# A hybrid block on one core: eight row products on TensorE in four modulation blocks, one scaling on ScalarE, and the roots of both LRU directions side by side

## The chip, the core and the metric

The kernel runs on one core of a Trainium2 chip. Five engines of that core work in parallel, each in the order of its own queue: TensorE (PE; its weight loads are counted as PEld), VectorE (DVE), ScalarE (ACT), GpSimd (POOL) and SyncE (SP), which issues most of the transfers. The metric is the device time of one execution in microseconds.

## The reference, cut to what matters

One layer, sequence 1024, model width 1024, batch 1, all in float32. `c` gives six modulation vectors; the first two, shift and scale, act on the normalised input.

```python
mod = jnp.dot(jax.nn.silu(c), w_mod[l]) + b_mod[l]
shift1, scale1, gate1, shift2, scale2, gate2 = jnp.split(mod[:, None, :], 6, axis=-1)
h = rms_norm(x, g_norm1[l]) * (1.0 + scale1) + shift1
proj = jnp.dot(h, w_in[l])
x_lru, z_lru, q, k, v = jnp.split(proj, SPLITS, axis=-1)
xc = conv(x_lru)                                  # 4 taps along the sequence
h_fwd = rg_lru(xc, w_a[0], ..., reverse=False)
h_bwd = rg_lru(xc, w_a[1], ..., reverse=True)
y_lru = (h_fwd + h_bwd) * jax.nn.gelu(z_lru)
y_att = diff_attention(q, k, v, ...)              # q and k are rms-normed per head first
x = x + gate1 * jnp.dot(jnp.concatenate([y_lru, y_att], -1), w_out[l])
x = x + gate2 * expert_choice_ffn(rms_norm(x, g_norm2[l]) * (1 + scale2) + shift2, ...)
```

The recurrence of one direction is `h = a * h_before + u`, with two gates `r` and `i` from block-diagonal products:

```python
log_a = LRU_C * r * jax.nn.log_sigmoid(lam)
a = jnp.exp(log_a)
u = jnp.sqrt(-jnp.expm1(2.0 * log_a)) * (i * xc)
```

## The kernel before

Products in float32 are made of rounded parts: `hh` and `hl` are the high and low part of a block of `h`, `w..h` and `w..l` those of a weight, and each product is three passes (high by high, high by low, low by high).

**The front.** The 1024 columns of `h` are cut into eight blocks of 128. For block k, shift and scale are a product of the 1024 values of `silu(c)` with 256 columns of `w_mod`, loaded as two tiles `wm` of four rows of weights each. `m_mm(k)` lets PE do the first `RP[k]` of the eight row products, into the PSUM tile `mp`. `m_sum(k)` brings the rest in on DVE: with `RP[k] == 8` one COPY of `mp` to `acc` (L303), otherwise four products with addition (L305), of which the last writes `acc`. `m_red(k)` sums `acc` over the partitions on PE (tile `pm`), `m_col(k)` makes the columns `acol` and `shc` of it (L315, L317), and `h_make(k)` scales: `hh` on ACT, the plain scaling (`h_2` for block 2) on DVE (L326) where k is in `KH` and else on ACT, and the difference `hl` (L329), on POOL for all blocks but the last. `x_mm` multiplies the blocks with the first 256 columns of `w_in` into `pjx`. The order of PE, DVE and ACT in this stretch is that in which the code is written (a manual schedule): `m_mm(k + 2)` and `m_sum(k + 2)`, the products of block k, then `m_red`, `m_col` and `h_make` of block k + 2.

**The LRU.** From `pjx` the convolution makes tiles `xc` (one for 128 channels, four in all, indexed by ct), and `do_lru(ct)` does both directions of one: `xch` and `xcl`, the parts of `xc`; gates `pg` on PE and `tg` on ACT (Tanh); `tt` (Tanh), the decay `a` in place in the first `tg` (Exp) and its Square `sqa` on ACT; two products on DVE (L515, L516); then for each direction the root of `tt` on ACT, a product on POOL (L521, out `tg`) and a scan over the sequence on DVE (L523 forward, L525 backward), and at last the addition of both (L528). Here a scheduler orders each engine's instructions. Whenever the next function on ACT is not in the loaded set, an ACT_TABLE_LOAD stands ahead of it.

**Between them** run the q and k projections, `proj_qk`: a projection `pjq` or `pjk` on PE; its Square `sqk` on ACT, a reduction `rk` on DVE (L578), a root on ACT, a reciprocal (L580) and a product `nk` (L582) on DVE, and then eight transposes of `nk` on PE (`pbk`, L589), from which `hk` on ACT and `lk` on DVE (`hq` and `lq` for q, L596) follow. The projections' weights are split: `wi_0h`, `wi_1h` on ACT, `wi_0l`, `wi_1l` on POOL or DVE (L142). The PSUM pools of `pj` and of `pg` have two tiles each, so a projection can begin only when the one before the last has been read.

**After that** come attention, the output projection, and the experts, which take the second half of the time.

Of the kernel before, what the change touches and what calls it, by code (L numbers as in the profile page):

```python
# [12 lines left out]
AF = mybir.ActivationFunctionType  # L13
# [44 lines left out]
KS0 = 1  # L58
KLT = 4
KM = 3  # L60
RP = (8, 8, 4, 4, 4, 4, 4, 4)
KW = 7
KV = (7,)
KH = (0, 1, 2, 7)
KB = (0, 1, 2, 7)
CAP = 128
RPAD = 56
# [15 lines left out]
def tile_block(ctx: ExitStack, tc, x, cols, w_mod, b_mod, w_in, wa, wx, lam_qk, relT, w_out, g2, w_router,  # L83
# [5 lines left out]
    def act(out, in_, func=AF.Copy, **kw):  # L89
        return A.activation(out=out, in_=in_, func=func, **kw)  # L90

    def mm(out, lhsT, rhs, start, stop):
        return T.matmul(out, lhsT=lhsT, rhs=rhs, start=start, stop=stop)  # L93
# [46 lines left out]
    def split(src, hi, lo, eng=None):  # L140
        act(hi, src)
        return (eng or V).tensor_tensor(out=lo, in0=src, in1=hi.bitcast(F32), op=ALU.subtract)  # L142
# [151 lines left out]
    def m_mm(k):  # L294
        mps[k] = psb.tile([P, 2, P], F32, tag="pj", bufs=2, name=f"mp{k}")
        for r in range(RP[k]):
            g = 32 * (r % 4)
            mm(mps[k][g:g + 32], scz[:, r, :], wm[k, r // 4][:, r % 4], r < 4, r + 4 >= RP[k])

    def m_sum(k):  # L300
        accs[k] = sm1.tile([P, 2, P], F32, tag="acc", bufs=4, name=f"acc{k}_0")
        if RP[k] == KT:
            V.tensor_copy(accs[k], mps[k])  # L303
        for r in range(RP[k], KT):
            V.scalar_tensor_tensor(out=accs[k] if r == KT - 1 else mps[k], in0=wm[k, r // 4][:, r % 4], scalar=sc[:, r:r + 1],  # L305
# [13 lines left out]
    def h_make(k):  # L319
# [4 lines left out]
        i_ = act(a, xT[k], AF.Identity, scale=ac, bias=sh)  # L324
        if k in KH:
            V.tensor_scalar(out=b32, in0=xT[k], scalar1=ac, scalar2=sh, op0=ALU.mult, op1=ALU.add)  # L326
# [116 lines left out]
    def lt_(name, shape=None, dt=F32):  # L443
        return lru.tile(shape or [P, S], dt, tag="l", bufs=NL, name=name)
# [46 lines left out]
    def do_lru(ct):  # L491
        xc = xc_[ct]
        xh = lt_(f"xch{ct}", None, F32R)
        xl = lt_(f"xcl{ct}", None, F32R)
        split(xc, xh, xl, V if ct in LV else G_)
        hs, st = [], []
        for d in range(2):
            pre = []
            for gi in range(2):
                pg = psb.tile([P, 1024], F32, tag="pg", bufs=2, name=f"pg{ct}_{d}_{gi}")  # L500
                i = d * 4 + ct
                for wi_, (w_, xv) in enumerate(((bdh, xh), (bdl, xh), (bdh, xl))):
                    for n in range(2):
                        mm(pg[:, n * 512:(n + 1) * 512], w_[gi][:, i, :], xv[:, n * 512:(n + 1) * 512], wi_ == 0, wi_ == 2)
                tg = lt_(f"tg{ct}_{d}_{gi}")
                act(tg, pg, AF.Tanh, scale=0.5, bias=hb[:, gi * 8 + i:gi * 8 + i + 1])
                pre.append(tg)
            ta, ti = pre
            i = d * 4 + ct
            tt = lt_(f"tt{ct}_{d}")  # L510
            act(tt, ta, AF.Tanh, scale=nkap[:, i:i + 1], bias=nkap[:, i:i + 1])
            act(ta, ta, AF.Exp, scale=kap[:, i:i + 1], bias=kap[:, i:i + 1])
            sq = lt_(f"sqa{ct}_{d}")
            act(sq, ta, AF.Square)
            V.scalar_tensor_tensor(out=tt, in0=sq, scalar=1.0, in1=tt, op0=ALU.add, op1=ALU.mult)  # L515
            tis.append(V.scalar_tensor_tensor(out=ti, in0=ti, scalar=1.0, in1=xc, op0=ALU.add, op1=ALU.mult))  # L516
            st.append((ta, ti, tt))
        for d in range(2):
            ta, ti, tt = st[d]
            act(tt, tt, AF.Sqrt, scale=0.25)  # L520
            G_.tensor_tensor(out=ti, in0=ti, in1=tt, op=ALU.mult)  # L521
            if d == 0:
                V.tensor_tensor_scan(out=tt, data0=ta, data1=ti, initial=0.0, op0=ALU.mult, op1=ALU.add)  # L523
            else:
                V.tensor_tensor_scan(out=tt[:, ::-1], data0=ta[:, ::-1], data1=ti[:, ::-1], initial=0.0,  # L525
                                     op0=ALU.mult, op1=ALU.add)
            hs.append(tt)
        V.tensor_tensor(out=hs[0], in0=hs[0], in1=hs[1], op=ALU.add)  # L528
        hs_[ct] = hs[0]
# [112 lines left out]
    mod_rest(0, 1)  # L642
    behind.reverse()
    do_lru(0)
    wq1 = load_in(1280, G_)
    mod_rest(0, 2)
# [3 lines left out]
    mod_rest(0, 4)  # L650
    proj_qk(wq1, 0, 1)
    do_lru(1)
    mod_rest(0, 5)
    wz0 = load_in(512, G_)
# [35 lines left out]
    mod_rest(1, 4)  # L690
    behind.append(convs[1])
    proj_v(wv0, 0, vt[0:2], lambda _: do_lru(2), VA)
    mod_rest(1, 5)
    behind.append(tis[-1])
# [786 lines left out]
```

## Time and the profile before

| | |
|---|---|
| Time, median of 3 runs | 1165.89 us (1162.89 to 1166.04) |
| The profiled execution: time, span | 1167.24 us, 1165.5 us |
| Busy share of the span: PE, PEld, DVE, ACT, POOL | 96%, 80%, 82%, 68%, 39% |
| Mean granted clock of TensorE | 0.978 |
| Waits of PE from 20 to 320 us | 2.2, 2.0 and 1.2 us, and three of 0.4 us or less |

The span is counted from the first instruction to the last. Times in the rows are microseconds from the start of the span, unless they are marked otherwise. A granted clock of 1.0 is full speed (2.4 GHz), 0.50 is half. In a timeline, rows of equal form that follow each other are put together (x3), and in brackets stands how long the engine was idle before, and what ended that.

### The profile page before, as it was taken

The page shows a single profiled execution, that of the slowest core. Times are in us where ns is not written, and L with a number is a line of the kernel's source. Part 1 is how long each engine was busy: PE and PEld are TensorE (multiplying, and loading weights), DVE is VectorE, ACT ScalarE, POOL GpSimd, SP SyncE. Part 2 cuts the span into 40 slices and gives each one's busy share as a digit, 9 for nine tenths or more (in the row PEclk, how much of TensorE's full clock was granted, in tenths as well). Part 3 has the DMA queues.
Part 4 walks back from the last instruction along what each step waited for, and adds up shares of the span by engine and source line. Part 5 has one row for each costly group of instructions (what it writes and reads, how often), then busy time and mean ns, then how long its engine had stood idle before and what let it go on. Part 6 is the DMA issues. An engine that isn't in the chain of part 4 may idle for free.

```text
span 1165.5 us, 17852 instructions
## 1 busy us (share of the span) xinstructions
PE 1113.3 (96%) x6303; PEld 935.2 (80%) x6303; DVE 960.6 (82%) x1258; ACT 795.1 (68%) x1051; POOL 457.9 (39%) x528
## 2 busy tenths in 40 slices
PE   5999999999999999999379999999999999999996
PEld 4799998888899998777358888888888888888885
DVE  7686767884699995655779999999999999999995
ACT  7539382384588785543448888787888787888784
POOL 5683331133144463553634332444332444332410
PEclk9899999999999999999679999999999999999998
DMA  9753637615684217336889999999999999999911
GB/s 338 232 167 106 238 106 252 218 37 130 197 227 104 76 37 255 127 127 217 309 313 326 394 394 383 393 391 387 397 394 392 367 391 403 400 392 386 389 33 18
DMA packets 146992, 304.33 MB, mean 261 GB/s; under 512 B 16972, under 2 KB 43724, under 8 KB 146900
## 3 DMA queue, kind: packets, MB, share of 16 engines
q1 hardware_dynamic: 135008, 279.99, 66.4%
q0 software_dynamic: 5488, 19.45, 6.4%
q10 hardware_dynamic: 6408, 3.77, 1.1%
q8 instruction: 49, 0.80, 0.3%
q14 instruction: 39, 0.32, 0.1%
HBM read 277.95 MB, written 25.21 MB: 260 GB/s over the span
## 4 chain that ended last, share of the span: by engine, by line
PE 88%; DVE 4%; issue 3%; SPq 2%; DMA 1%; ACT 1%; POOLq 0%; POOL 0%; DVEq 0%; ACTq 0%
PE ab L93 28%; PE y L93 14%; PE mix L93 7%; PE pv L93 5%; PE sc L93 5%; PE pjk L93 4%; PE pjv L93 4%; PE pjz L93 4%; PE pjx L93 4%; PE pjq L93 3%; PE pw L820 2%; PE pg L93 2%; SPq L288 1%; PE pf L1365 1%; PE pe L1274 1%
## 5 line engine op out<-in xcount | busy, mean ns | idle before, releaser
L1265 POOL TENSOR_SCALAR oh<-iot,slot 128x128 bf16<-128x128 bf16 x120 | 144.1, 1215 | 252.3 <-PE pf L1365 252.3
L93 PE MATMUL ab<-wh,xeh 128*128 128x512 f32 x512 | 202.2, 395 | 0.3 <-ACT xeh L90 0.3
L93 PE MATMUL ab<-wh,xel 128*128 128x512 f32 x512 | 199.6, 390 | 0.0
L93 PE MATMUL ab<-wl,xeh 128*128 128x512 f32 x512 | 157.7, 389 | 0.0
L93 PEld LDWEIGHTS ab<-wl,xeh 128*128 128x128 f32 x512 | 96.1, 188 | 20.4
L93 PEld LDWEIGHTS ab<-wh,xel 128*128 128x128 f32 x512 | 96.2, 188 | 19.4 <-DVE xel L1278 0.5
L93 PEld LDWEIGHTS ab<-wh,xeh 128*128 128x128 f32 x512 | 96.0, 188 | 19.5 <-ACT xeh L90 0.5
L142 DVE TENSOR_TENSOR wl<-w_0r,wh 128x1024 fp32r<-128x1024 f32 x79 | 96.9, 1226 | 10.5 <-ACT wh L90 0.4
L90 ACT ACTIVATE wh<-w_0r 128x1024 fp32r<-128x1024 f32 x81 | 85.9, 1062 | 24.3 <-PE ab L93 14.9
L142 DVE TENSOR_TENSOR wl<-w_3r,wh 128x1024 fp32r<-128x1024 f32 x79 | 96.7, 1224 | 6.3
L90 ACT ACTIVATE wh<-w_1r 128x1024 fp32r<-128x1024 f32 x79 | 83.6, 1059 | 23.0 <-PE ab L93 18.8
L90 ACT ACTIVATE wh<-w_3r 128x1024 fp32r<-128x1024 f32 x79 | 83.9, 1063 | 22.2 <-PE ab L93 17.4
L142 DVE TENSOR_TENSOR wl<-w_2r,wh 128x1024 fp32r<-128x1024 f32 x80 | 96.3, 1220 | 2.4 <-ACT wh L90 1.1
L90 ACT ACTIVATE wh<-w_2r 128x1024 fp32r<-128x1024 f32 x80 | 84.8, 1060 | 19.7 <-PE ab L93 17.8
L142 DVE TENSOR_TENSOR wl<-w_1r,wh 128x1024 fp32r<-128x1024 f32 x78 | 92.5, 1219 | 3.6 <-ACT wh L90 1.6
L774 DVE CUSTOM_DVE_ANT_0 p<-sc,bias 128x1024 f32<-128x1024 f32 x64 | 77.8, 1217 | 10.7 <-PE sc L93 10.6
L93 PE MATMUL y<-wh,htl 128*128 128x512 f32 x256 | 82.9, 395 | 0.0
L93 PE MATMUL y<-wh,hth 128*128 128x512 f32 x256 | 81.1, 396 | 0.0
L93 PE MATMUL y<-wl,hth 128*128 128x512 f32 x256 | 79.5, 391 | 0.0
L90 ACT ACTIVATE p<-p,stat 128x1024 f32<-128x1024 f32 x60 | 68.4, 1151 | 0.3 <-DVE stat L774 0.3
L93 PEld LDWEIGHTS pv<-v,wt 128*128 128x128 f32 x512 | 61.7, 192 | 2.5
L93 PE MATMUL pv<-v,wt 128*128 128x128 f32 x512 | 62.1, 275 | 0.0
(466 smaller groups left out, 2843.8 us busy)
## 6 DMA issues: line engine op xcount, KB each, us to landing
w_0r<-in_w_dram SPq DMA_DIRECT2D x81, 512.0 KB, 5.0
w_1r<-in_w_dram SPq DMA_DIRECT2D x79, 512.0 KB, 5.9
w_2r<-in_w_dram SPq DMA_DIRECT2D x78, 512.0 KB, 6.0
w_3r<-in_w_dram SPq DMA_DIRECT2D x77, 512.0 KB, 8.9
wr<-in_w_mod_dram SPq DMA_DIRECT2D x32, 512.0 KB, 4.4
wi<-in_w_in_dram SPq DMA_DIRECT2D x18, 512.0 KB, 3.4
w_5r<-in_w_dram SPq DMA_DIRECT2D x17, 512.0 KB
wm<-in_w_mod_dram SPq DMA_DIRECT2D x32, 256.0 KB, 4.4
```

The lines of the kernel that those rows point to most:

```text
L90: return A.activation(out=out, in_=in_, func=func, **kw)
L93: return T.matmul(out, lhsT=lhsT, rhs=rhs, start=start, stop=stop)
L142: return (eng or V).tensor_tensor(out=lo, in0=src, in1=hi.bitcast(F32), op=ALU.subtract)
L288: lds.append(SY.dma_start(out=w[:, :, g, :], in_=w_mod[rh * 512:(rh + 1) * 512, c0:c0 + P].rearrange("(r p) c -> p r c", p=P)))
L774: V.tensor_tensor_reduce(out=p_, in0=scp[g, j], in1=prs[h][0][:, b0:b0 + S], op0=ALU.add, op1=ALU.min, scale=1.0, scalar=3.0e38, accum_out ...
L820: T.transpose(pw[:, b * P:(b + 1) * P], pt_[g, 0][:, kt * P:(kt + 1) * P], ident)
L1265: G_.tensor_scalar(out=oh[:, t, :], in0=iot, scalar1=slot[:, e, t:t + 1], scalar2=None, op0=ALU.is_equal)
L1274: T.transpose(pt[:, b * P:(b + 1) * P], xe[:, (kq * 4 + b) * P:(kq * 4 + b + 1) * P], ident)
L1365: T.transpose(pt[:, b * P:(b + 1) * P], sa[:, b * P:(b + 1) * P], ident)
```

## The change

There are three edits. `RP` is 8 for blocks 2 and 3 too, so PE does all eight row products of these and DVE copies. `KH` loses block 2, so ACT makes its plain scaling. In `do_lru` the roots of both directions are issued after the Square of the second direction.

```diff
-RP = (8, 8, 4, 4, 4, 4, 4, 4)
+RP = (8, 8, 8, 8, 4, 4, 4, 4)
 KW = 7
 KV = (7,)
-KH = (0, 1, 2, 7)
+KH = (0, 1, 7)
...
             sq = lt_(f"sqa{ct}_{d}")
-            act(sq, ta, AF.Square)
+            i_sq = act(sq, ta, AF.Square)
             V.scalar_tensor_tensor(out=tt, in0=sq, scalar=1.0, in1=tt, op0=ALU.add, op1=ALU.mult)
...
         for d in range(2):
             ta, ti, tt = st[d]
-            act(tt, tt, AF.Sqrt, scale=0.25)
+            with tc.issue_after(i_sq.ins):
+                act(tt, tt, AF.Sqrt, scale=0.25)
             G_.tensor_tensor(out=ti, in0=ti, in1=tt, op=ALU.mult)
```

On DVE, at the front, the order changes as follows (`mp_430` belongs to block 2, `mp_461` or `mp_462` to block 3; a line without a sign is in both).

```order
 L326 TENSOR_SCALAR h_1_418<-xT_121,acol,shc 128x1024
-L305 SCALAR_TENSOR_TENSOR mp_430<-wm_1_222,sc,mp_430 128x256 x3
-L305 SCALAR_TENSOR_TENSOR acc_0_435<-wm_1_222,sc,mp_430 128x256
-L315 SCALAR_TENSOR_TENSOR acol<-pm_444,bs_112,col 128x1
-L317 TENSOR_TENSOR shc<-pm_444,col 128x1
-L326 TENSOR_SCALAR h_2_451<-xT_121,acol,shc 128x1024
-L305 SCALAR_TENSOR_TENSOR mp_461<-wm_1_228,sc,mp_461 128x256 x3
-L305 SCALAR_TENSOR_TENSOR acc_0_466<-wm_1_228,sc,mp_461 128x256
```

```order
+L303 COPY acc_0_439<-mp_430 128x256
+L315 SCALAR_TENSOR_TENSOR acol<-pm_445,bs_112,col 128x1
+L317 TENSOR_TENSOR shc<-pm_445,col 128x1
+L303 COPY acc_0_471<-mp_462 128x256
+L315 SCALAR_TENSOR_TENSOR acol<-pm_481,bs_112,col 128x1
+L317 TENSOR_TENSOR shc<-pm_481,col 128x1
```

Each block has one copy in place of four products, and `h_2` has left the engine; on PE `mp` gets four more matmuls (two `x4` rows where one stood) in each of these blocks, and ACT gets `h_2` behind `hh` of block 2.

On DVE at the first LRU tile (`tt_0` forward, `tt_1` backward; from here on a line of the changed kernel is one higher) the order before was this.

```order
L523 SCALAR_TENSOR_TENSOR tt_0_1025<-tg_0_0_1014,tg_0_1_1023 128x1024
L578 TENSOR_REDUCE rk_0_1181<-sqk_0_1179 128x16
L515 SCALAR_TENSOR_TENSOR tt_1_1050<-sqa_1_1053,tt_1_1050 128x1024
L580 RECIPROCAL rk_0_1181<-rk_0_1181 128x16
L582 TENSOR_TENSOR nk_0_1185<-pjk_0_1082,rk_0_1181 128x1024
L525 SCALAR_TENSOR_TENSOR tt_1_1050<-tg_1_0_1039,tg_1_1_1048 128x1024
L596 SCALAR_TENSOR_TENSOR lq_1_1198<-pbq_1_1188,gqk,hq_1_1197 128x1024
L528 TENSOR_TENSOR tt_0_1025<-tt_0_1025,tt_1_1050 128x1024
```

Now it is this.

```order
L515 SCALAR_TENSOR_TENSOR tt_1_1052<-sqa_1_1055,tt_1_1052 128x1024
L524 SCALAR_TENSOR_TENSOR tt_0_1027<-tg_0_0_1016,tg_0_1_1025 128x1024
L526 SCALAR_TENSOR_TENSOR tt_1_1052<-tg_1_0_1041,tg_1_1_1050 128x1024
L579 TENSOR_REDUCE rk_0_1183<-sqk_0_1181 128x16
L529 TENSOR_TENSOR tt_0_1027<-tt_0_1027,tt_1_1052 128x1024
L581 RECIPROCAL rk_0_1183<-rk_0_1183 128x16
L583 TENSOR_TENSOR nk_0_1187<-pjk_0_1084,rk_0_1183 128x1024
L597 SCALAR_TENSOR_TENSOR lq_1_1200<-pbq_1_1190,gqk,hq_1_1199 128x1024
```

The second scan and the addition now stand ahead of `nk_0`, and the second scan ahead of the reduction `rk_0` too. The second tile's DVE rows change in the same way.

On ACT at the first tile the order before was this (a row without names is a table load; `tg_1_0` takes the exponential, `tt_0` and `tt_1` the roots).

```order
L90 ACTIVATE tt_1_1050<-tg_1_0_1039,nkap 128x1024
L90 ACT_TABLE_LOAD
L90 ACTIVATE tt_0_1025<-tt_0_1025 128x1024
L90 ACT_TABLE_LOAD
L90 ACTIVATE tg_1_0_1039<-tg_1_0_1039,kap 128x1024
L90 ACTIVATE sqk_0_1179<-pjk_0_1082 128x1024
L90 ACTIVATE sqa_1_1053<-tg_1_0_1039 128x1024
L90 ACTIVATE xch_1594<-xc_700 128x1024
L90 ACT_TABLE_LOAD
L90 ACTIVATE rk_0_1181<-rk_0_1181,misc 128x16
L90 ACTIVATE tt_1_1050<-tt_1_1050 128x1024
L90 ACTIVATE hq_1_1197<-pbq_1_1188,gqk 128x1024
```

Now it is this.

```order
L90 ACTIVATE tt_1_1052<-tg_1_0_1041,nkap 128x1024
L90 ACTIVATE tg_1_0_1041<-tg_1_0_1041,kap 128x1024
L90 ACTIVATE sqa_1_1055<-tg_1_0_1041 128x1024
L90 ACT_TABLE_LOAD
L90 ACTIVATE tt_0_1027<-tt_0_1027 128x1024
L90 ACTIVATE tt_1_1052<-tt_1_1052 128x1024
L90 ACTIVATE sqk_0_1181<-pjk_0_1084 128x1024
L90 ACTIVATE xch_1596<-xc_702 128x1024
L90 ACTIVATE rk_0_1183<-rk_0_1183,misc 128x16
L90 ACTIVATE hq_1_1199<-pbq_1_1190,gqk 128x1024
```

One load stands ahead of both roots where three stood around them; over the four tiles nine loads go. On POOL the product of the second direction (L521) now stands ahead of `xcl`, the low part of the next tile's `xc`, at the first and the third tile, where `xcl` stood between the two products. SP's order is unchanged.

## Rows read from the trace of the kernel before

**Rows 1.** The page of the profile, part 1: busy time, share of the span, instructions.

```profile
PE 1113.3 (96%) x6303; PEld 935.2 (80%) x6303; DVE 960.6 (82%) x1258; ACT 795.1 (68%) x1051; POOL 457.9 (39%) x528
```

**Rows 2.** The page, part 4: the chain that ended last, by engine.

```profile
PE 88%; DVE 4%; issue 3%; SPq 2%; DMA 1%; ACT 1%; POOLq 0%; POOL 0%; DVEq 0%; ACTq 0%
```

**Rows 3.** Waits of PE from 20 to 320 us: what for, total us, times, longest.

```profile
PE pg L93 <- ACT tg L90: 2.2, 1, 2.2
PE pm L93 <- DVE acc L305: 2.0, 2, 1.5
PE pbk L589 <- DVE nk L582: 1.2, 1, 1.2
...
PE pjq L93 <- POOL wi_1l L142: 0.3, 1, 0.3
```

**Rows 4.** Stretches: window, length, busy us (instructions) of PE PEld DVE ACT POOL, PEclk, DMA share, GB/s.

```profile
32.06:42.30 10.24, 9.78 (x32) 6.69 (x31) 5.04 (x11) 3.83 (x4) 5.13 (x3) 0.50 1.13 342
...
253.93:257.34 3.41, 3.41 (x9) 2.64 (x9) 3.41 (x3) 3.35 (x4) 0.67 (x1) 0.50 0.02 5
```

**Rows 5.** Timeline of PE, front: start, us, line, operation, count [idle before].

```profile
30.25 0.61 PE L93 MATMUL pm<-ones,acc 128*128 128x1 f32 x4 [1.53 <-DVE acc L305]
...
42.27 0.52 PE L93 MATMUL pm<-ones,acc 128*128 128x1 f32 x4
...
46.17 0.50 PE L93 MATMUL pm<-ones,acc 128*128 128x1 f32 x4
46.60 0.64 PE L93 MATMUL mp<-wm,scz 128*32 128x256 f32 x8
...
60.73 0.28 PE L93 MATMUL pjq<-wi_0h,hh 128*128 128x256 f32 x1
```

**Rows 6.** Timeline of DVE, front.

```profile
24.00 0.42 DVE L303 COPY acc<-mp 128x256 f32<-128x256 f32 x1
...
28.16 1.53 DVE L305 SCALAR_TENSOR_TENSOR mp<-wm,sc,mp 128x256 f32<-128x256 f32 x3
```

**Rows 7.** Timeline of ACT, first LRU tile.

```profile
99.81 1.28 ACT L90 ACT_TABLE_LOAD   x1
101.10 1.06 ACT L90 ACTIVATE tt<-tt 128x1024 f32<-128x1024 f32 x1
```

**Rows 8.** Timeline of POOL, first LRU tile.

```profile
102.24 2.38 POOL L521 TENSOR_TENSOR tg<-tg,tt 128x1024 f32<-128x1024 f32 x1 [13.07 <-ACT tt L90]
...
114.68 2.40 POOL L142 TENSOR_TENSOR wi_1l<-wi,wi_1h 128x1024 fp32r<-128x1024 f32 x1
117.03 4.39 POOL L142 TENSOR_TENSOR wi_0l<-wi,wi_0h 128x1024 fp32r<-128x1024 f32 x1
```

**Rows 9.** Timeline of DVE, first LRU tile.

```profile
104.66 2.29 DVE L523 TENSOR_TENSOR_SCAN tt<-tg,tg 128x1024 f32<-128x1024 f32 x1 [4.74 <-POOL tg L521]
106.86 1.20 DVE L578 TENSOR_REDUCE rk<-sqk 128x16 f32<-128x1024 f32 x1
...
111.34 1.23 DVE L582 TENSOR_TENSOR nk<-pjk,rk 128x1024 f32<-128x1024 f32 x1
114.77 4.46 DVE L525 TENSOR_TENSOR_SCAN tt<-tg,tg 128x1024 f32<-128x1024 f32 x1 [2.21 <-POOL tg L521]
```

**Rows 10.** Timeline of PE, first LRU tile.

```profile
114.28 1.04 PE L589 MATMUL pbk<-ident,nk 128*128 128x128 f32 x8
```

**Rows 11.** Timeline of ACT, second LRU tile.

```profile
160.76 1.25 ACT L90 ACTIVATE tg<-tg,kap 128x1024 f32<-128x1024 f32 x1
```

**Rows 12.** Timeline of DVE, second LRU tile.

```profile
168.78 1.23 DVE L582 TENSOR_TENSOR nk<-pjk,rk 128x1024 f32<-128x1024 f32 x1 [0.45 <-DMA qkd<-lq]
```

**Rows 13.** Timeline of PE, second LRU tile.

```profile
171.54 0.63 PE L93 MATMUL pjz<-hh,wi_0h 128*128 128x512 f32 x2
```

**Rows 14.** Timeline of POOL, third LRU tile.

```profile
243.45 3.18 POOL L142 TENSOR_TENSOR xcl<-xc,xch 128x1024 fp32r<-128x1024 f32 x1 [2.58 <-issue]
```

**Rows 15.** Timeline of PE, third LRU tile.

```profile
247.89 0.62 PE L93 MATMUL pg<-xcl,bdh 128*128 128x512 f32 x2
```

## The prediction

> **What bounds the kernel now.** I read the page first: TensorE (PE) is busy for 96% of the span [rows 1] and 88% of the chain that ended last lies on it [rows 2]. So time is won or lost only where PE waits or runs at a lower clock. The waits of PE from 20 to 320 us, the stretch that holds all three edits, are few [rows 3]: 2.0 us for the DVE sum of a modulation block (`acc`, L305), 2.2 for a gate activation, 1.2 for a normalised k tile (`nk`, L582). The table of stretches adds the clock [rows 4]: it is granted at 0.50, the 1.2 GHz level, from 32.06 to 42.30, and again from 253.93 to 257.34. Both stretches come soon after a wait of PE: 1.53 us before 30.25 [rows 5], and the 2.2 us one [rows 3]. At half rate 10.24 us of work is 5.1 us lost, and 3.41 us is 1.7 lost. Then I read each engine's timeline at the front and around the first LRU tile.
>
> **The front (blocks 2 and 3).** Removed: for each block four DVE products, three in 1.53 us and a last one [rows 6], until PE gets its sum at 30.25 [rows 5]. Added: one COPY per block, 0.42 us [rows 6], and eight matmuls per block on PE; eight take 0.64 us by the row [rows 5], but overlap with their neighbours, so I take 0.5 (bounds 0.45 and 0.64), 1.0 for both blocks. The copy can start where the first product stood, at 28.16 [rows 6], and ends near 28.7, when PE, which went idle 1.53 before 30.25 [rows 5], now still has the added matmuls in front of it. So both `pm` waits, 2.0 us [rows 3], go. The scaling `h_2` moves from DVE to ScalarE (ACT), one pass of about 1.2 us, as the exponential of the same size takes [rows 11]. Its consumer `hl` is multiplied one block later, some 3.9 us on, the step from 42.27 to 46.17 [rows 5]; that covers it, and if the cover failed it would cost at most the pass. Without the idle 1.53 I expect no drop of the clock, so the 5.1 us come back too. Front: -2.0 - 5.1 + 1.0 = **-6.1**. If the clock drops all the same, at most -1.0 is left.
>
> **The roots, as an edit on ACT.** The order has nine table loads fewer, at 1.28 us each [rows 7], 11.5 us of ACT. But the waits list has one wait of PE for ACT there, the 2.2 [rows 3]; elsewhere this relief shortens nothing. What decides is what the roots release. The first root, at 101.10, now comes after the exponential and the Square of the second direction. The removed load begins at 99.81 [rows 7]: exponential 1.25 [rows 11] to 101.06, Square (taken as 1.06, like the root) to about 102.15, load 1.28, so the root starts at 103.45 and ends at 104.5, and the second root ends at 105.5. GpSimd's (POOL's) first product starts at 104.6 instead of 102.24 [rows 8]. Both products can now run back to back, and on DVE both scans stand ahead of the reduction `rk_0`, the reciprocal and `nk_0` for which PE waits next.
>
> The price hangs on one thing that the rows show: a DVE scan and a POOL product exclude each other. The scan takes 2.29 us alone and 4.46 when it is issued at 114.77, just behind `wi_1l` (114.68 to 117.08); `wi_0l`, issued at 117.03, then takes 4.39 instead of 2.40, since it waits for that scan [rows 8, 9]. The two engines take turns, an operation each. So: `tg_0` 104.6 to 107.0; POOL's second product is ready at that moment and goes first, to 109.35; first scan (2.2) to 111.5; POOL's `xcl` (2.2) to 113.7; second scan to 115.9; reduction (1.20) to 117.0; the add of both directions (taken as 1.2, like the reduction) while ACT takes the small root; reciprocal to 118.4; `nk_0` (1.23) to 119.7. Before, `nk_0` ended at 112.57 [rows 9], and PE took it at 114.28 [rows 10]. PE stalls for 119.7 - 114.3 = 5.4 us. Behind ACT's `rk_0` root, which waits for the reduction, stand `hq_1`, `wi_1h` and `wi_0h`, three passes of about 1.06; they end by about 120.5, when PE, released at 119.7, comes to them. The 1.2 us wait for the second `nk` and the 0.3 for `wi_1l` [rows 3] vanish in the stall: -1.5. A stall of that length I charge with the clock loss after the 2.2 us wait, 1.7 (bounds 0, as behind the 1.2 us wait no stretch at half clock came, and 5.1, as at the front). Tile 0: 5.4 - 1.5 + 1.7 = **+5.6**.
>
> Beside these rows stands the Trainium skill, page "SBUF — State Buffer", section "SBUF: two separate sides": a VectorE operation with two SBUF inputs and a GpSimd operation that reads SBUF hold one port pair for the whole instruction, and the other blocks fully. The pair of 4.46 and 2.29 agrees. Another page of the Trainium skill, "Advanced Engine Details and Errata", section "VectorE Performance Modes", names only two-port modes as interfering; by it the scans would not be held, which is the faster rival below, and the 4.46 speaks against it.
>
> **The second tile** repeats it. Its second exponential starts at 160.76 [rows 11], behind two loads and a root that no longer stand there, so it goes to 157.1; with `hq_1`, the Square and the one load behind it the first root comes at about 161.6 and ends at 162.7; products to 165.2 and 167.5; scans to 169.7 and, POOL having nothing to put between, 171.9; reduction 173.0, add 174.2, reciprocal and `nk_0` to 175.7, where it ended at 170.01 [rows 12]. PE's `pjz` takes over the bank that `nk_0` reads at 171.54 [rows 13]: stall 4.2, and 1.7 of clock: **+5.9**.
>
> **Third and fourth tile.** On POOL `xcl` of the fourth tile now stands behind both products, and takes turns with scans. It ran from 243.45 for 3.18 us, to 246.63 [rows 14], and PE wanted it at 247.89 [rows 15]. From a root 2.4 us later, product, product, scan and `xcl` put its end near 251.2: a stall of 3.3. The old wait of 2.2 [rows 3] is then absorbed, and its clock loss stays. **+1.1** (bounds: -3.5, if `xcl` gets in early and wait and clock loss go; +3, if the clock falls longer). DMA issues are not reordered, so no queue of SP is passed.
>
> **Sum** against the profiled execution, whose span of 1165.5 is 1167.24 with what lies around it: -6.1 + 5.6 + 5.9 + 1.1 = +6.5, so 1173.7. That execution is 1.35 above the median of 1165.89; against the median the forecast is **1172.4 us**.
>
> **Rivals.**
> *Faster: the scans are not held up.* If the first scan wins its turn against the second product and nothing else is blocked, `nk_0` of tile 0 ends near 115.4 (reduction, reciprocal and `nk_0` right behind scans at 107.0 and 109.35), a stall of 1.1 that the 1.5 of later waits give back; tile 1 stalls about 2 without a clock loss; tiles 2 and 3 win 3.5. -6.1 - 0.4 + 2.2 - 1.5 = -5.8: **about 1160**. For it: ACT is relieved of 11.5 us, and PE's queue between may be slack. Against it: the 4.46 and 4.39 [rows 8, 9]. It decides once both `nk_0` end within 2 us of PE's demand. The Trainium skill, page "ScalarE: Activation LUTs", section "Table sets: the hidden batching unit", favours it: calls should be batched by table set, at some 2.7 us per switch; nine of those would be an estimated 24 us of ACT, against 11.5 by the row.
> *Cancelling.* One of the two q/k stalls is absorbed by slack behind it or brings no clock loss; the front pays for the rest: +6.5 - 6 = about 0, **1166**.
> *The front's clock falls anyway*, because something else than the wait lowers it: -1.0 instead of -6.1, **1177.5**. For it: the drop came 1.8 us after the wait's end, not at it; against it: both drops shown follow a wait [rows 3, 4, 5].
>
> **How the numbers follow.** Main case 0.58 (own range 1169 to 1176), front's clock 0.07, cancelling 0.18, faster 0.17. A measurement of this kernel tells 0.3%, 3.5 us, from no change, so faster means below 1162.4 and slower above 1169.4. The range leaves out most of the faster case and the end of the high one: 1161 to 1178. Slower 0.65, same 0.18, faster 0.17.
>
> **What would show it.** Right: no wait of `pm` for DVE and clock 1.0 from 32 to 42; `pjq` some 6 us earlier than at 60.73 [rows 5]; then waits of PE of 4 to 5.5 us for `nk` (`pbk`) and for the bank before `pjz`, with half clock behind them, scans of 4.4 us, and a wait for `xcl`. Wrong: waits for `nk` under 2 us, scans of 2.3 us beside POOL products, or half clock again near 32.

## The result and the profile after

The changed kernel takes 1174.12 us in the median (1173.07 to 1176.12, 4 runs), the kernel before 1165.22 (1162.89 to 1166.04, 4 runs). The ratio is 1.0082, 95% interval 1.0060 to 1.0103: 9 us slower, where 1172.4 was forecast, 6.5 more than the median of three runs known then. The profiled execution, from which the rows of this section come, took 1176.12.

The waits of PE from 20 to 320 us in the changed kernel, to be set against [rows 3]:

```profile
PE pbk L590 <- DVE nk L583: 5.3, 1, 5.3
PE pjz L93 <- DVE nk L583: 4.0, 1, 4.0
PE pg L93 <- POOL xcl L142: 3.2, 1, 3.2
PE pt L263 <- DVE xT L276: 0.3, 1, 0.3
```

The wait of `pm` for DVE is gone, and so are the 2.2 for a gate and the 0.3 for `wi_1l`. Three new ones stand at the places that the prediction named. The stretches show the clock; columns as in [rows 4]:

```profile
32.00:42.30 10.30, 10.30 (x68) 7.72 (x68) 6.79 (x17) 7.51 (x7) 8.13 (x4) 1.00 1.14 345
113.80:119.15 5.35, 5.35 (x25) 5.35 (x26) 4.49 (x5) 2.70 (x4) 4.33 (x2) 0.50 0.65 214
175.77:180.67 4.90, 4.90 (x12) 3.84 (x13) 4.43 (x5) 0.72 (x2) 1.86 (x2) 0.51 0.34 109
```

At the front the clock is at full speed where it was 0.50. Behind the two long waits it is at half for 5.35 and 4.90 us, and behind the wait for `xcl` from 259.1 to 262.5. On PE's timeline the stretch behind the first two blocks now runs without a gap. Blocks 2 and 3 have 16 matmuls into `mp` where 8 stood, so eight more each, as the prediction counts them (the text on the change says four). `pjq` starts 5.95 earlier than in [rows 5]:

```profile
27.09 1.07 PE L93 MATMUL mp<-wm,scz 128*32 128x256 f32 x16
...
29.12 0.50 PE L93 MATMUL pm<-ones,acc 128*128 128x1 f32 x4
...
36.36 0.50 PE L93 MATMUL pm<-ones,acc 128*128 128x1 f32 x4
...
54.78 0.28 PE L93 MATMUL pjq<-wi_0h,hh 128*128 128x256 f32 x1
```

The first LRU tile on DVE and on POOL, to be set against [rows 8, 9]:

```profile
101.12 4.47 DVE L524 TENSOR_TENSOR_SCAN tt<-tg,tg 128x1024 f32<-128x1024 f32 x1 [3.64 <-POOL tg L522]
105.51 4.42 DVE L526 TENSOR_TENSOR_SCAN tt<-tg,tg 128x1024 f32<-128x1024 f32 x1
109.85 1.19 DVE L579 TENSOR_REDUCE rk<-sqk 128x16 f32<-128x1024 f32 x1
110.97 1.21 DVE L529 TENSOR_TENSOR tt<-tt,tt 128x1024 f32<-128x1024 f32 x1
...
112.43 1.23 DVE L583 TENSOR_TENSOR nk<-pjk,rk 128x1024 f32<-128x1024 f32 x1
```

```profile
98.67 4.77 POOL L522 TENSOR_TENSOR tg<-tg,tt 128x1024 f32<-128x1024 f32 x2 [15.44 <-ACT tt L90]
103.40 4.39 POOL L142 TENSOR_TENSOR xcl<-xc,xch 128x1024 fp32r<-128x1024 f32 x1
113.41 2.38 POOL L142 TENSOR_TENSOR wi_1l<-wi,wi_1h 128x1024 fp32r<-128x1024 f32 x1 [5.62 <-ACT wi_1h L90]
```

Both scans take 4.4 us instead of 2.3: the first waits for the second product (98.67 to 103.44, two in a row), `xcl` waits for the first scan and holds up the second. `nk_0` ends at 113.66. In the second tile, where POOL has nothing behind its products, the first scan is held up and the second is not, and that is the same operation on tiles of the same size in the same kernel:

```profile
162.80 4.77 POOL L522 TENSOR_TENSOR tg<-tg,tt 128x1024 f32<-128x1024 f32 x2 [16.31 <-ACT tt L90]
...
165.25 4.48 DVE L524 TENSOR_TENSOR_SCAN tt<-tg,tg 128x1024 f32<-128x1024 f32 x1 [3.39 <-POOL tg L522]
169.65 2.26 DVE L526 TENSOR_TENSOR_SCAN tt<-tg,tg 128x1024 f32<-128x1024 f32 x1
...
174.40 1.23 DVE L583 TENSOR_TENSOR nk<-pjk,rk 128x1024 f32<-128x1024 f32 x1
```

Following the first matmul of each tile's product on PE through both traces gives the balance, as start after less start before: `pjq` -5.95; `pbq` of the third q tile, behind the first LRU tile, +0.06; the fourth `pbk`, behind the second, +6.43; the first attention scores, behind all four, +7.45. So the front gave 6.0, and the tiles took 6.0, 6.4 and 1.0. Between the scores and the end another 1.4 is added, most of it near 600 and 640 us. In the run with the roots alone (below) only 0.1 comes in there, so it seems to belong to this one execution, which was the slowest of the four.

### The profile page after: what moved, and what is told of

Read it like the earlier page. It is cut to its first block, busy times and chain, and to the rows that moved or that the text cites. A ratio compares the mean times of both kernels' runs of the same rounds, so it can differ in the third digit from the quotient of the medians.

```text
span 1174.4 us, 17874 instructions
## 1 busy us (share of the span) xinstructions
PE 1115.1 (95%) x6319; PEld 938.3 (80%) x6319; DVE 961.2 (82%) x1251; ACT 785.0 (67%) x1043; POOL 461.4 (39%) x528
## 4 chain that ended last, share of the span: by engine, by line
PE 77%; DVE 3%; issue 3%; POOL 1%; DMA 1%; POOLq 0%; ACT 0%; DVEq 0%; ACTq 0%
PE ab L93 28%; PE y L93 13%; PE mix L93 7%; PE pv L93 5%; PE sc L93 5%; PE pjz L93 4%; PE pjv L93 4%; PE pw L821 2%; PE pjx L93 2%; PE pf L1366 1%; PE pe L1275 1%; PE pg L93 1%; DVE junk L1153 1%; POOL oh L1266 1%; PE ph L1063 1%
```

## Experiments

Each ratio is against the kernel before, run on the same chip in the same session; medians of different sessions are not to be compared. Waits that the kernel before has too, as that of 1.2, are left out of the table.

| kernel | waits of PE for `nk_0` of the first LRU tile, for `nk` of the second, for `xcl` | median us | ratio, 95% interval |
|---|---|---|---|
| the change | 5.3, 4.0, 3.2 | 1174.12 | 1.0082, 1.0060 to 1.0103 |
| front edits alone | none, none, none | 1159.50 | 0.9971, 0.9959 to 0.9983 |
| eight row products alone | the same | 1161.13 | 0.9972, 0.9961 to 0.9984 |
| roots alone | 5.3, 4.0, 3.2 | 1177.17 | 1.0119, 1.0103 to 1.0134 |
| change, second scan late | 0.3, 1.2, 3.2 | 1165.95 | 1.0012, 1.0003 to 1.0021 |
| change, products on DVE | 2.9, 1.6, none | 1162.33 | 0.9986, 0.9977 to 0.9996 |
| change, wait filled | 0.7 and 4.7 of filler, 4.0, 3.2 | 1171.62 | 1.0056, 1.0040 to 1.0071 |
| before, front's wait filled | none, none, none (1.9 for `pm`) | 1163.34 | 1.0005, 0.9992 to 1.0018 |
| front, roots in tiles 3 and 4 | none, none, none | 1161.36 | 0.9974, 0.9962 to 0.9985 |
| all roots, queues mended | 0.3, 1.2, none | 1162.97 | 0.9990, 0.9979 to 1.0001 |

**The two halves of the change.** The front edits without the roots, and the roots without the front edits:

```diff
-            with tc.issue_after(i_sq.ins):
-                act(tt, tt, AF.Sqrt, scale=0.25)
+            act(tt, tt, AF.Sqrt, scale=0.25)
```

```diff
-RP = (8, 8, 8, 8, 4, 4, 4, 4)
+RP = (8, 8, 4, 4, 4, 4, 4, 4)
-KH = (0, 1, 7)
+KH = (0, 1, 2, 7)
```

> The two front edits alone (eight row products on TensorE for blocks 2 and 3, the plain scaling of block 2 on ScalarE), the roots as before. Theory (the front gives 6.0 us, the roots take it back and more): 1159 us, 0.995 of before; no wait of pm, granted clock 1.0 from 32 to 42, and every matmul from the first pjq to the mixture of experts 6 us earlier than before. Rival (the front's gain is lost again behind it, because the weights of the projections or the LRU's tiles are not ready 6 us sooner): 1163 to 1166, with new waits of PE between 60 and 300 us.

> The roots of both directions together, the front as before. Theory: the loss of the LRU stands by itself, 6.0 in the first tile, 6.4 in the second, 1.0 in the third and fourth: 1178.5 us, with waits of PE of 5.3 and 4.0 us for nk and 3.2 for xcl. Rival (the stalls come only because PE arrives 6 us earlier than what feeds it): 1166 to 1170, with waits below 2 us.

The halves add up: 0.9971 and 1.0119 are 3.4 us won and 13.9 lost, 10.5 together, against 9.5 for the change (interval 7 to 12). The roots alone show the waits of 5.3, 4.0 and 3.2, though PE is not 6 us early there; the rival falls. The front alone has only the old waits of [rows 3] behind it, so nothing loses its gain again; but that gain is 3.4 (interval 2.0 to 4.8), not 6.0.

The half clock behind the two long waits was shorter in the profile of the roots alone than in that of the change:

```profile
118.10:121.00 2.90, 2.90 (x14) 2.90 (x15) 2.27 (x2) 1.61 (x4) 2.90 (x2) 0.50 0.54 201
```

It lasted to 121.1 here, and from 179.2 to 182.6 in the second tile: 3.0 and 3.4 us of work at 0.50, so 1.5 and 1.7 lost, where the change's profile has 2.7 and 2.4. Set against the third profile of the kernel before (below), in which the clock also fell behind the 2.2 us wait, the tiles cost 5.0, 5.7 and 1.1 by PE's starts, where the change's profile has 6.0, 6.4 and 1.0. So these costs differ by up to 1 us from one execution to the next, though the waits are the same.

**What the front is worth.** The kernel before, profiled twice more, unchanged:

> The kernel before, unchanged, profiled once more. Theory 1 (the half clock from 32 to 42 us belongs to the wait at 30.25 in every execution): the same stretch at 0.50 again, and a time near that of the first profile, 1166 to 1167. Theory 2 (behind such a wait the half clock comes in some executions and not in others; the first profile, at 1167.2, was one of those with it, and the median is mixed): no or a shorter stretch at half clock, and 1162 to 1164.

> The kernel before, unchanged, profiled a third time. Theory (how long the half clock lasts behind the wait at 30.25 differs between executions): a stretch at half clock at the front of another length than 10.2 or 3.8 us, or none, and a time between 1162 and 1167 that goes with it. Rival (it is 10.2 us as a rule and the second profile was the exception): 10 us, 1166 to 1167.

Stretches of the first of these two, columns as in [rows 4]:

```profile
31.85:35.27 3.42, 3.42 (x16) 2.21 (x16) 2.95 (x5) 1.24 (x1) 2.73 (x2) 0.50 1.08 315
35.30:42.30 7.00, 6.84 (x44) 4.80 (x44) 4.23 (x13) 4.49 (x4) 3.94 (x2) 1.00 1.06 314
```

In both the half clock at the front lasts 3.4 us (in the second from 31.95 to 35.35, at 0.50) and not 10.2, and the times are 1163.42 and 1163.45 against 1167.24. The second and the third agree, so 10.2 us is not the rule and the rival falls. The profile of the roots alone, whose front is that of before, differs again: there the clock fell only behind the wait for block 3, from 35.8 to 39.2. Counted from the first `pm`, `pjq` starts after 38.6, 35.5 and 35.3 us in the three profiles of before and after 37.0 with the roots alone, so two of four lost time behind 35.3 us, 3.2 and 1.6. In the third profile the half clock behind the 2.2 us wait of [rows 3] came again, in the second it did not, so what follows a wait of 1.5 or 2.2 us differs from one execution to the next. The next run shows what the 3.4 us cost:

```diff
-        pms[k] = psb.tile([P, 2], F32, tag="pg", bufs=2, name=f"pm{k}")
+        pms[k] = psb.tile([P, 512], F32, tag="pg", bufs=2, name=f"pm{k}")
+        if k == 2:
+            for _ in range(6):
+                mm(pms[k], hh[0][:, 0:P], hh[0][:, 0:512], True, True)
```

> The kernel before, with six matmuls whose result is not used put ahead of the sum pm of block 2, 1.4 us on TensorE in the place of its wait of 1.5 us; nothing else is changed, and VectorE still makes its four products. Theory (the half clock from 32 to 42 us follows the idle time): the clock stays at 1.0 there, and although no work is saved the time falls by about 5: 1160 us. Rival (the clock falls for another reason): half clock stays and the time is 1165 to 1166.

PE's timeline of this run, and below it two stretches:

```profile
28.57 1.55 PE L93 MATMUL pm<-hh 128*128 128x512 f32 x6
30.25 0.61 PE L93 MATMUL pm<-ones,acc 128*128 128x1 f32 x4
...
35.40 0.58 PE L93 MATMUL pm<-ones,acc 128*128 128x1 f32 x4 [1.94 <-DVE acc L305]
...
39.35 0.50 PE L93 MATMUL pm<-ones,acc 128*128 128x1 f32 x4
```

```profile
28.57:35.40 6.83, 4.76 (x27) 3.07 (x26) 5.74 (x11) 1.24 (x1) 4.76 (x3) 1.00 1.12 332
35.40:42.30 6.90, 6.90 (x45) 5.20 (x46) 4.23 (x12) 5.50 (x5) 2.76 (x2) 1.00 1.12 345
```

The clock stays at 1.00, as the theory had it, and the time stays too, as the rival had it (1.0005). The wait of 1.94 us before 35.40 explains both: with the clock at full speed PE is done with block 2 sooner and waits for DVE's products of block 3, which end when they ended before; `pjq` starts 35.7 us after the first `pm`, no sooner than in the second and third profile. So up to about 35 us DVE's products set the pace, and the clock did not matter there. The forecast had taken wait and half clock for two prices.

**The scaling on ScalarE.** The eight row products without it:

```diff
-KH = (0, 1, 7)
+KH = (0, 1, 2, 7)
```

> The eight row products alone; the plain scaling of block 2 stays on VectorE and the roots as before. Theory (the scaling is covered on either engine): as with both front edits, 1159.5 us within 1 us, and no wait of pm. Rival (on VectorE the scaling, which takes 1.8 us beside GpSimd, delays the copy of block 3): a wait of pm of 0.5 to 1.5 us, 1160.5 to 1164.

0.9972 against 0.9971, and the same waits. The move to ACT neither costs nor brings anything that these runs can tell; the rival's wait of `pm` does not come.

**Queue order or exclusion.** Exclusion means that a scan and a GpSimd operation hold each other up. Each of two kernels takes one of the two away. In the first, the second direction of the first two tiles is written behind `nk_0`: a function `scan(d)` holds the product, the scan and the addition of a direction, and `late` holds the call until `proj_qk` has issued `nk_0`:

```diff
...
+        scan(0)
+        if ct < 2:
+            late.append(lambda: scan(1))
+        else:
+            scan(1)
...
+            while kind and late:
+                with tc.issue_after(behind[-1].ins):
+                    late.pop()()
```

> The changed kernel, but in the first two tiles the second direction's product, its scan and the addition are written behind nk_0 of the k projection, so that on VectorE the reduction, the reciprocal and nk_0 stand ahead of the second scan. Theory (what costs is that nk_0 is queued behind both scans): nk_0 ends 3.5 to 4 us sooner in each tile, though the first scan still takes 4.4 us beside GpSimd's product; PE waits under 1 us for each; the time is the front's gain plus the 1.0 of the third tile, 1160 to 1162 us. Rival 1 (what costs is the later first root, 2.4 us, with the exclusion): the stalls stay at 2 us or more and the time is 1166 to 1169. Rival 2 (a second place waits in its stead, as the weights wi behind the scans): 1164 to 1168 with a new wait of PE.

DVE's and POOL's timelines of the first tile in this run, and below them PE's waits:

```profile
100.90 4.46 DVE L528 TENSOR_TENSOR_SCAN tt<-tg,tg 128x1024 f32<-128x1024 f32 x1 [3.64 <-POOL tg L526]
105.29 1.19 DVE L588 TENSOR_REDUCE rk<-sqk 128x16 f32<-128x1024 f32 x1
...
107.20 1.23 DVE L592 TENSOR_TENSOR nk<-pjk,rk 128x1024 f32<-128x1024 f32 x1
108.34 2.28 DVE L530 TENSOR_TENSOR_SCAN tt<-tg,tg 128x1024 f32<-128x1024 f32 x1
...
111.71 2.15 DVE L532 TENSOR_TENSOR tt<-tt,tt 128x1024 f32<-128x1024 f32 x1
```

```profile
98.46 4.77 POOL L526 TENSOR_TENSOR tg<-tg,tt 128x1024 f32<-128x1024 f32 x2 [15.45 <-ACT tt L90]
103.18 4.39 POOL L142 TENSOR_TENSOR xcl<-xc,xch 128x1024 fp32r<-128x1024 f32 x1
```

```profile
PE pg L93 <- POOL xcl L142: 3.2, 1, 3.2
PE pjq L93 <- POOL wi_1l L142: 1.6, 1, 1.6
PE pjz L93 <- DVE nk L592: 1.2, 1, 1.2
...
PE pbk L602 <- DVE nk L592: 0.3, 1, 0.3
```

On POOL nothing has moved: the scheduler still put the second direction's product right behind the first. What moved is DVE's part, so this run tests the queue order of DVE alone. `nk_0` now ends at 108.43, 5.2 sooner than in the change, although the first scan takes 4.46 as before. The waits for `nk` fall from 5.3 and 4.0 to 0.3 and 1.2. Rival 2 has a part: PE waits 1.6 for `wi_1l`, which now takes turns with the late scan and the addition. By PE's starts the first tile costs 0.5 and the second 2.2, where they cost 6.0 and 6.4; the wait for `xcl` is untouched, and from within it on, in this execution, the clock was at half (246 to 253 us). At 1.0012, some 1165, the time is above the forecast 1160 to 1162.

In the second, queue order stays and GpSimd's products go to DVE:

```diff
-            G_.tensor_tensor(out=ti, in0=ti, in1=tt, op=ALU.mult)
+            V.tensor_tensor(out=ti, in0=ti, in1=tt, op=ALU.mult)
```

> The changed kernel with both products of the LRU (the ones ahead of the scans) on VectorE in place of GpSimd, in all tiles. nk_0 is still queued behind both scans; only GpSimd's products, which the scans take turns with, are gone. Theory (queue order and exclusion both count): in the second tile, where GpSimd then has nothing left, both scans take 2.2 to 2.3 us, nk_0 ends some 2.3 us sooner and PE's wait of 4.0 falls to about 1.7; in the first tile, where xcl is still between, one scan or xcl is held up and the wait falls from 5.3 to about 3.2; 1167 to 1170 us in all. Rival 1 (the exclusion is no part of the cost): products and scans one behind the other on VectorE, waits as long as before or longer, 1174 or more. Rival 2 (the exclusion is all of it): no waits for nk, 1161.

DVE's timeline of both tiles in this run, with POOL's `xcl` of the first between them:

```profile
100.66 2.29 DVE L524 TENSOR_TENSOR_SCAN tt<-tg,tg 128x1024 f32<-128x1024 f32 x1
102.86 4.43 DVE L526 TENSOR_TENSOR_SCAN tt<-tg,tg 128x1024 f32<-128x1024 f32 x1
```

```profile
101.24 3.91 POOL L142 TENSOR_TENSOR xcl<-xc,xch 128x1024 fp32r<-128x1024 f32 x1 [18.24 <-ACT xch L90]
```

```profile
157.67 2.36 DVE L522 TENSOR_TENSOR tg<-tg,tt 128x1024 f32<-128x1024 f32 x2 [0.90 <-ACT tt L90]
159.94 2.29 DVE L524 TENSOR_TENSOR_SCAN tt<-tg,tg 128x1024 f32<-128x1024 f32 x1
162.15 2.27 DVE L526 TENSOR_TENSOR_SCAN tt<-tg,tg 128x1024 f32<-128x1024 f32 x1
...
166.91 1.23 DVE L583 TENSOR_TENSOR nk<-pjk,rk 128x1024 f32<-128x1024 f32 x1
```

The products take 1.2 us each on DVE, and both scans of the second tile take 2.3; in the first tile one scan is still held up, by `xcl`. The waits are 2.9 and 1.6 where 3.2 and 1.7 were expected, 2.4 shorter each. Nearly all of that is the one hold-up of 2.2 that is gone in each tile, as the first scan is issued only 0.2 sooner: 3.4 us behind the start of the first root (97.29 and 156.57) and not 3.6 (97.53 and 161.66 in the change). Behind these waits the clock stays at full speed, `xcl` is no longer late, and the time is 1162.33, under the 1167 that was expected, since a clock loss and the third tile's wait had been left in.

Both causes are needed. Against the front alone the roots cost 12.9 us in the change (1.0082 against 0.9971); the other queue order on DVE gives back some 8 of them and the removal of GpSimd's products some 11, each with the other cause left in place. The second figure contains the wait for `xcl`, which went with GpSimd's products, and the clock that no longer fell; by PE's starts the first two tiles cost 1.2 and 1.7 there.

**The clock behind the stall.** Filler in the wait for the first `nk`, in the changed kernel:

```diff
+                if n == "k0_0":
+                    for _ in range(20):
+                        mm(pb[:, 0, :], hh[0][:, 0:P], hh[0][:, 0:512], True, True)
```

> The changed kernel with twenty matmuls whose result is not used ahead of the transposes of the first k tile, 4.6 us of TensorE in the place of its wait of 5.3 us. No work is saved and nk_0 comes no sooner. Theory (the stall costs its own length and then about 2.8 us at half clock, 5.6 us at 0.50): no half clock behind 113 us, the first tile costs 3.2 us less, 1171.3 us. Rival (the loss is the wait alone): 1174.

PE's timeline of this run around the filler and the transposes:

```profile
108.56 4.72 PE L93 MATMUL pbk<-hh 128*128 128x512 f32 x20
113.94 1.09 PE L593 MATMUL pbk<-ident,nk 128*128 128x128 f32 x8 [0.66 <-DVE nk L583]
```

PE begins the transposes no sooner, but it was busy until 0.66 before them; from 108.5 to 119 the granted clock is 1.00, and by PE's starts the first tile costs 3.5 instead of 6.0. The ratio falls by 0.0026, some 3 us, but the intervals of the two kernels overlap, so it is the trace that speaks against the rival: `nk_0` ends no sooner, and 2.5 us are won behind it. The second stall, not filled, still has its half clock (172.9 to 179.7).

**Is there a version in which the roots together pay?** The first of these kernels has a function `cut(ct)` that makes `xch` and `xcl`: `cut(3)` splits the fourth tile ahead of the third tile's products, and only tiles three and four have their roots together; in the second all four have, with the late second direction in the first two.

```diff
...
+        if ct == 2:
+            cut(3)
         for d in range(2):
             ta, ti, tt = st[d]
-            with tc.issue_after(i_sq.ins):
+            with tc.issue_after(i_sq.ins) if ct > 1 else ExitStack():
```

> The front edits; the roots together only in the third and fourth tile, and the low part xcl of the fourth tile issued ahead of the third tile's two products on GpSimd. Theory (there the roots together are good once xcl is not behind the products, since ScalarE reaches the next gates sooner): the wait of PE of 2.2 us for a gate falls below 1, no wait for xcl, and 1157 to 1158.5 us against 1159.5 with the front alone. Rival (the wait moves on to another tile of the chain): 1159 to 1160, with a new wait near 245 to 262 us.

> The roots together in all four tiles, with the second direction of the first two tiles behind nk_0 (as in the late scan) and xcl of the fourth tile ahead of the third tile's products (as in the run with the third and fourth tile alone), and the front edits. Theory (both prices of the roots are queue order and can be taken away, and nine table loads fewer then bring nothing, as PE does not wait for ScalarE): 1160 to 1163 us, the time of the front edits alone within 2 us, no wait for xcl, waits of 1.2 to 1.7 us in the first two tiles. Rival (the relief of ScalarE by 11.5 us pays once the queues are right): below 1158.

In the first the waits of 2.2 and for `xcl` are both gone, and by PE's starts 2.5 us are won where the gates are needed. Then 0.9 and 0.7 are lost behind them, at 252.4 to a `tg` on ACT and at 255.6 to `s2w`, and at the first attention scores 0.3 is left of the 2.5. The ratio to the kernel before (0.9974) is that of the front alone (0.9971); the rival with the moved wait holds. In the second there is no wait over 1.6 us left, with 16 table loads from 60 to 311 us where the kernel before has 25. It is still no faster than the front alone (0.9990): the first two tiles cost 2.7 by PE's starts, the 2.5 at the gates are won, and the same two waits take most of them away again. So nine loads fewer, 11.5 us of ACT, buy no time in any of these versions. No kernel is faster than the one with the front edits alone (0.9971); those with 0.9972 and 0.9974 cannot be told from it.

## Why the prediction was right

**The front: right in kind, too large.** The waits went, the clock stayed up and `pjq` came 5.95 earlier, all against the first profile. Against the two later profiles of before (`pjq` at 58.81 and 57.64, with the first `pm` at 23.36 and 22.34, where it is at 22.24 in the changed kernel) the gain is 2.8 to 2.9, and the measured one is 3.4. The term that was mis-sized is "the 5.1 us come back too". The half clock behind 35.3, 7.0 us of [rows 4] and 3.5 of the 5.1, was not there in the two later profiles, and with the roots alone it cost 1.6: it differs between executions. The 1.6 ahead of that do come back, but as DVE's pace and not as the clock: there the sum of block 3 would have been late at either level. The eight added matmuls cost 0.4 a block, near the 0.5 charged.

**The first tile: right.** Waits of 5.3 against 5.4 forecast, a cost of 6.0 against 5.6. The chain was right step by step (first root, products back to back, a scan of 4.4, `xcl` between the scans), with `nk_0` at 113.66, which is 119.6 on the old time scale, against 119.7. The loss of clock was 2.7 (5.35 us at 0.50) in this profile and 1.5 in that of the roots alone, on either side of the 1.7 charged. The two later waits vanished as said.

**The second tile: right.** A wait of 4.0 against 4.2, a cost of 6.4 against 5.9; the clock 2.4 here and 1.7 with the roots alone, against 1.7.

**Third and fourth tile: right.** A wait of 3.2 for `xcl` against 3.3, 1.0 against 1.1 in all, and the half clock behind it stayed, as said.

With the front at 3.4 the terms give -3.4 + 6.0 + 6.4 + 1.0 = +10.0 by the tiles of the change's profile and -3.4 + 5.0 + 5.7 + 1.1 = +8.4 by those of the roots alone, and 9 was measured. So the forecast of 6.5 was low because of the front's term; the tiles were priced within what two executions show. The faster rival failed at the step where the scans are not held up: they took 4.47 and 4.42 beside GpSimd's work in the first tile of the change, and 2.29 and 2.27 in the second tile of the run that had taken that work away. The exclusive lock of the Trainium skill's page "SBUF — State Buffer", section "SBUF: two separate sides", agrees with these four numbers. That rival's sum also has a slip: it counts 1.5 won in the third and fourth tile, where its own text says 3.5; with 3.5 it is near 1158, and the result lies far from either. No run shows that ACT's relief shortens the whole. The Trainium skill, page "ScalarE: Activation LUTs", section "Table sets: the hidden batching unit", says to batch calls by table set; the traces agree that this saves loads (25 become 16, 1.28 us each), and no run shows that it saves time here. The cancelling case did not come: both stalls cost about what was charged, clock loss included.

## What to carry to other kernels

Before you take out table loads, ask which engine waits for ScalarE, and look at what is queued behind the instruction that moves. Here the second scan came to stand ahead of the reduction that TensorE needed next, and both scans were lengthened by GpSimd's work beside them; taking away either one gave back most of the loss. On an engine that runs its queue in order, put what feeds the bound engine first, and see whether a GpSimd operation beside it makes it longer. And do not charge the clock of one profile in full: profile the kernel before a second time, and ask of each slow stretch whether another engine set the pace in it anyway.

## What the runs showed of the hardware

What follows a wait differs between executions of the same kernel: behind the 1.5 us wait at the front the clock was at half for 10.2, 3.4 and 3.4 us, and not at all in the profile of the roots alone, where it fell behind the next wait, of 1.7. Behind the 2.2 us one it was at half in two of three profiles of the kernel before and in that of the eight row products alone, and not in those of the front alone and of the front's wait filled. Behind 2.9 and 1.6 us (products on DVE) it did not fall; with 5.3 and 4.0 it fell each time unless the wait was filled, five of five in three kernels, and with the 3.2 for `xcl` in four of four. In the run with the products on DVE a wait of 0.9 us near 256 had one behind it. With the waits of 5.3 and 4.0 it fell before they were over in four of the five, at 112.4 in the change, while PE waited until 113.80, and once 0.1 us after the end, at 179.2 with the roots alone. What decides the shorter ones, and how long the half clock lasts, stays open.

In the rows shown VectorE's scans and GpSimd's operations take turns, an operation each: a scan issued while a GpSimd product or `xcl` had just started took 4.4 to 4.5 us, and 2.3 with nothing beside it.
